# A gate group's copy moved ahead of its multiplication, top-k steps re-paced, and norm sums paired by column half, in a two-layer decoder on one core

## The chip, the cores and the metric

The kernel runs on one core of a Trainium2 chip. The metric is the device time of one execution in microseconds (us). The kernel before takes 2584.49 us, the median of 3 runs (2582.99 to 2586.38).

## The reference, cut to what matters

Two layers work on 256 tokens of 1024 features, all in float32. Each layer has a mixer (attention, a gated recurrence and retention, merged by gates and one output projection) and then PEER, a retrieval over 128 x 128 single-neuron experts. Each ends in a norm: `x = layer_norm(alpha * x + f(x))`, with mean and variance over the 1024 features of a token.

PEER computes `q = x @ wq`, scores it against two sets of 128 keys, takes the top 16 of each and the top 16 of the 256 sums, and weighs them by softmax. That gives, for each token and each of 8 heads, 16 expert numbers e and gates g. The output is `y = sum over (head, k) of gelu(U[e] . x) * g * V[e]`.

The kernel does not gather. It computes `gelu(U x)` for all 16384 experts, multiplies by a dense gate matrix G (expert by token, mostly zero), and multiplies by V.

## The kernel before, in words

**Jobs and splits.** The weights are cut into 408 jobs a layer, 128 x 1024 numbers (512 KB) each. `run` (line 498) goes through them in order. For a job it first prepares the weight of two jobs later (`ensure_split(i + LA)`, LA = 2): SyncE loads it to `raw` (4 buffers), ScalarE casts the high part `wh` (line 250), VectorE subtracts for the low part `wl` (line 259; for some mixer jobs partly GpSimd). `wh` and `wl` have 3 buffers each. Then it issues the job's matmuls (`mm_t`, lines 301 to 308: 16 with `wh`, then 8 with `wl`), then side work (`pump`), then what `post` returns (for a U pair the gelu, line 1163). Every engine has its own queue, worked off in the order in which the program issued the instructions.

**Side work and its pacing.** Side work is written as generators. At each `yield c` a step ends that is charged c credits. `pump(b)` (line 283) adds the budget b to the class's credit (at most b + 2) and takes steps as long as the credit is above zero. `drain` issues all that is left at once. Which step falls under which job thus follows from charges and budgets alone.

**The stages of a PEER sublayer.** 16 Q jobs give the queries, 128 U jobs (U0 to U127) the activations, 128 V jobs (V0 to V127) the output. Under Q and U0 to U61 runs the class topk: `head` (line 975) and `finish` (line 991), whose last part transposes the chosen numbers on TensorE (lines 1034 to 1041), behind a last reduction (line 1028). After U61 stands `drain("topk")`, after U63 the memory of this work is released. Under U64 to U127 runs the class g: `gbuild` (line 1077) makes G, 8 tokens at a time, in 32 steps b. VectorE writes one-hot matrices (`onehots`, lines 1088 to 1092; two buffers of each). TensorE multiplies them into a PSUM pair of two banks (`accpair`, two pairs in all; lines 1114 and 1115, 16 matmuls, called a group here). `use` reads the pair twice: VectorE multiplies the first half of the experts into the ring of activations (line 1099), ScalarE copies the other half to `ge` (line 1101) and sends it to DRAM (line 1102) for `gback` to fetch in the V stage. `act_prep` (line 1143) splits two activations for the V jobs; the first one needs all 32 multiplications.

In each step b the order is

```
one-hots of b+1; group b; use(b-1): line 1099, line 1101, line 1102
```

**Sums and norm.** `body_o` (line 913) and `vjob`/`vmm` (lines 1179 to 1194) collect the result in four banks, [token half t][column half n]. `ln_flow` (line 351) issues the last products of a quarter, then `ln_part` (line 346): VectorE adds the quarter to the residual (line 348) and takes its statistics (line 349). Dependencies are tracked by tile, so the two halves of a pair count as one: a matmul into one half waits until a read of the other half, issued earlier, is over.

Of the kernel before, what the change touches and what calls it, by code (L numbers as in the profile page):

```python
# [169 lines left out]
def build(ctx: ExitStack, tc: tile.TileContext, I, out, layers=LAYERS, dbg=None):  # L170
# [18 lines left out]
    def nm(s):  # L189
        uid[0] += 1  # L190
        return f"{s}_{uid[0]}"

    def mmps():
        return ps.tile([P, 512], F32, tag="mm", name=nm("mm"), bufs=2)
# [4 lines left out]
    def accpair():  # L199

        return ps.tile([P, 1024], F32, tag="acc", name=nm("acc"), bufs=2)

    def accps2():
        a = accpair()
        return [a[:, 0:512], a[:, 512:1024]]
# [292 lines left out]
    def run(jobs, body, budget, late=None):  # L498

        for job in jobs:
            i = J["i"]
            assert allj[i][1] == job, (allj[i], job)
            if job != late:
                ensure_split(i + LA)
            h, lo = parts.pop(i)
            post = body(job, h, lo)
            if job == late:
                ensure_split(i + LA)  # L510
            pump(budget)
            if post is not None:
                post()
            J["i"] += 1


    def mixer(l, mp, xdram, xnext):
# [395 lines left out]
        def body_o(job, h, lo):  # L913
            n, k2 = job[1], job[2]
            if k2 == 0:
                for t, o in enumerate(accps2()):
                    V["o"][t][n] = o
            accs = [V["o"][0][n], V["o"][1][n]]
            if (n, k2) == (1, 3):
                ln_flow(lambda t, n: mm_n(accs, h, lo, V["mh"], V["ml"], k2, True, (t,)), [1], V["o"],  # L920
                        2.0 * ALPHA, X, sts, 4.0 * EPS, l, 0, gb, L8(), mp, xnext)
                return None
            mm_n(accs, h, lo, V["mh"], V["ml"], k2, k2 == 3)

            def post():
                for t in range(2):
                    ln_part(t, n, V["o"][t][n], 2.0 * ALPHA, X, sts)
            return post if k2 == 3 else None
# [6 lines left out]
    def peer(l, jobs, pp, ra, xdram, xnext):  # L935
        pos = [0]

        def take(n):
            r = jobs[pos[0]:pos[0] + n]
            pos[0] += n  # L940
            return r
# [49 lines left out]
        def finish():  # L991

            e = tp.tile([P, 2, 8, 16], F32, tag="e", name=nm("e"))
            sm = tp.tile([P, 2, 8], F32, tag="esum", name=nm("esum"))
            nc.vector.tensor_tensor(e, cv, cv[:, :, :, 0:1].to_broadcast([P, 2, 8, 16]), op=ALU.subtract)
            a = tp.tile([P, 2, 2, 128], U32, tag="ab", name=nm("ab"))
            cf = ci.rearrange("p t h k -> p t (h k)")
            nc.vector.tensor_scalar(a[:, :, 0, :], cf, 4, None, op0=ALU.logical_shift_right)
            nc.vector.tensor_scalar(a[:, :, 1, :], cf, 15, None, op0=ALU.bitwise_and)
            af = tp.tile([P, 2, 2, 8, 16], F16, tag="af", name=nm("af"))  # L1000
            nc.vector.tensor_copy(af, a.rearrange("p t f (h k) -> p t f h k", h=8))
            xf = tp.tile([P, 2, 2, 8, 16], F16, tag="xf", name=nm("xf"))
            nc.vector.tensor_copy(xf, i12)
            yield 1.9
            nc.scalar.activation(e, e, AF.Exp)
            yield 2.0
            nc.vector.tensor_reduce(sm, e, axis=AX.X, op=ALU.add)
            nc.vector.reciprocal(sm, sm)
            nc.vector.tensor_scalar(sm, sm, GSCALE, None, op0=ALU.mult)
            nc.vector.tensor_tensor(e, e, sm[:, :, :, None].to_broadcast([P, 2, 8, 16]), op=ALU.mult)  # L1010
            yield 1.3
            sel = tp.tile([P, 2, 2, 128], F32, tag="sel", name=nm("sel"))
            prev = None
            for t in range(2):
                for hf in range(2):
                    eq = tp.tile([P, 8, 16, 16], F16, tag="q8", name=nm("eq"), bufs=2)
                    sh = [P, 8, 16, 16]
                    nc.vector.tensor_tensor(eq, af[:, t, hf, :, :, None].to_broadcast(sh),
                                            iota[:, None, None, 0:16].to_broadcast(sh), op=ALU.is_equal)
                    yield 2.3  # L1020
                    xb = xf[:, t, hf, :, None, :].to_broadcast(sh)
                    nc.vector.tensor_tensor(eq, eq, xb, op=ALU.mult)
                    yield 1.2
                    if prev is not None:
                        nc.vector.tensor_reduce(prev[0], prev[1], axis=AX.X, op=ALU.add)
                        yield 2.3
                    prev = (sel[:, t, hf, :], eq.rearrange("p h k j -> p (h k) j"))
            nc.vector.tensor_reduce(prev[0], prev[1], axis=AX.X, op=ALU.add)
            dump(f"cv{l}", cv)
            dump(f"sel{l}", sel)  # L1030
            dump(f"e{l}", e)
            yield 2.3
            yield 1.0
            pt = sideps()
            for t in range(2):
                for hf in range(2):
                    nc.tensor.transpose(pt[:, (2 * hf + t) * P:(2 * hf + t + 1) * P], sel[:, t, hf, :], ident)
            nc.scalar.copy(idxT[:, 0:2, :], pt.rearrange("p (f t) -> p f t", f=2))
            pg = sideps()
            for t in range(2):  # L1040
                nc.tensor.transpose(pg[:, t * P:(t + 1) * P], e[:, t].rearrange("p h k -> p (h k)"), ident)
            nc.scalar.copy(idxT[:, 2, :], pg[:, :S])
            nc.vector.tensor_tensor(idxT[:, 3, :], pg[:, :S], idxT[:, 2, :], op=ALU.subtract)
            yield 0.4
# [23 lines left out]
                add_side("topk", head(ct // 2))  # L1068
            return post if q else None
        V["q"] = set()  # L1070
        run(take(16), body_q, 1.4, ("Q", 1))
        add_side("topk", finish())

        def gbuild():
            def onehots(c):

                B = pp.tile([P, 4, P, 2], F16, tag="ohB", name=nm("ohB"), bufs=2)  # L1080
                A = pp.tile([P, 2, 4, P, 2], F16, tag="act", name=nm("ohA"), bufs=2)
                sh = [P, 4, P, 2]

                def of(q):
                    return idxT[:, q, 8 * c:8 * c + 8].rearrange("p (a k) -> p a k", k=2)[:, :, None, :].to_broadcast(sh)

                io = iota2[:, None, :, :].to_broadcast(sh)
                nc.vector.tensor_tensor(B, io, of(1), op=ALU.is_equal)  # L1088
                nc.vector.tensor_tensor(A[:, 1], io, of(0), op=ALU.is_equal)
                yield 1.4  # L1090
                nc.vector.tensor_tensor(A[:, 0], A[:, 1], of(2), op=ALU.mult)  # L1091
                nc.vector.tensor_tensor(A[:, 1], A[:, 1], of(3), op=ALU.mult)
                yield 1.4
                return A, B

            def use(b, pg):
                pv = pg.rearrange("p (k i) -> p i k", k=8)
                r = RA[:, :, 8 * b:8 * b + 8]
                nc.vector.scalar_tensor_tensor(r, pv[:, 0:64, :], 1.0 / GSCALE, r, op0=ALU.mult, op1=ALU.mult)  # L1099
                ge = pp.tile([P, 64, 8], F32, tag="ge", name=nm("ge"), bufs=2)  # L1100
                nc.scalar.activation(ge, pv[:, 64:128, :], AF.Copy, scale=1.0 / GSCALE)  # L1101
                nc.scalar.dma_start(gd[l, b], ge.rearrange("p i k -> p (i k)"))  # L1102

            cur = yield from onehots(0)
            prev = None
            for b in range(S // 8):
                A, B = cur
                if b + 1 < S // 8:
                    cur = yield from onehots(b + 1)
                pg = accpair()  # L1110
                for k in range(8):
                    o = pg[:, P * k:P * k + P]
                    w = B[:, k // 2, :, k % 2]
                    mm(o, lhsT=w, rhs=A[:, 0, k // 2, :, k % 2], start=True, stop=False)  # L1114
                    mm(o, lhsT=w, rhs=A[:, 1, k // 2, :, k % 2], start=False, stop=True)
                if prev is not None:
                    use(b - 1, prev)
                prev = pg
                yield 0.7
            yield 0.5  # L1120
            use(b, prev)
            yield 0.7
            act_prep(0)

        def gback(s):
# [37 lines left out]
                nc.scalar.activation(ring[s][:, i - 1:i + 1, :], pt.rearrange("p (a t) -> p a t", a=2), AF.Gelu)  # L1163
            return post if q else None

        run(take(62), body_u, 1.6)
        drain("topk")
        run(take(2), body_u, 1.6)
        tp.release()
        V["rb"] = tc.alloc_tile_pool(name=nm("rb"), bufs=4, reuse_waits="tile")  # L1170
        credit["g"] = 0.0
        add_side("g", gbuild())
        run(take(64), body_u, 1.9)
        drain("g")
        act_prep(0)

        V["y"] = [accps2(), accps2()]

        def vmm(j, t, n, h, lo):
            a = acts[j // 2]  # L1180
# [103 lines left out]
```

## Time and profile before

| | us |
|---|---|
| median of 3 runs | 2584.49 |
| profiled execution, its own time | 2581.74 |
| span of the profile, first to last instruction | 2580.0 |
| TensorE busy, share of the span | 2499.6, 97% |
| VectorE busy | 1834.0, 71% |
| ScalarE busy | 1174.8, 46% |
| mean granted clock of TensorE | 0.993 |

A busy share says which engine sets the pace on the whole. Where an engine waits, the idle time before an instruction is put down to the instruction that released it. The timeline gives start and duration of each instruction; a matmul's duration overlaps the next one's, so the pace of matmuls is read from their starts.

### The profile page before, as it was taken

How to read it: one execution, taken by the hardware profiler on the slowest of the kernel's cores; microseconds unless marked ns; L12 is line 12 of the kernel's file. 1: busy time of each engine (PE TensorE's matmuls, PEld its weight loads, DVE VectorE, ACT ScalarE, POOL GpSimd, SP SyncE). 2: the span in 40 equal slices, each digit the busy share in tenths (PEclk: the TensorE clock that was granted, in tenths of full speed). 3: DMA queues.
4: the chain of work that ended last, by engine and by line, in shares of the span. 5: the costliest groups of instructions: out<-in, count | busy, mean ns of one | idle time of the engine just before them, and what ended most of it. 6: DMA issues, size and time to landing. Idle time of an engine off the chain costs nothing.

```text
span 2580.0 us, 43337 instructions
## 1 busy us (share of the span) xinstructions
PE 2499.6 (97%) x17428; PEld 2310.0 (90%) x17428; DVE 1834.0 (71%) x2736; ACT 1174.8 (46%) x1480; POOL 282.8 (11%) x263
## 2 busy tenths in 40 slices
PE   8999999999999999999999999999999999999998
PEld 7989998999999888888789999989999998888886
DVE  7886656888877756665588756568888777567655
ACT  5444444444444344444454444444444444444443
POOL 0822110200000000000028220111000000000000
PEclk9999999999999999999999999999999999999999
DMA  6445565555545458666554455655555555586663
GB/s 232 156 149 168 168 214 178 191 177 176 170 169 187 167 197 256 226 227 226 166 205 148 156 167 173 213 171 188 173 181 174 175 178 174 190 260 228 223 226 131
DMA packets 165913, 485.96 MB, mean 188 GB/s; under 512 B 15056, under 2 KB 47952, under 8 KB 165072
## 3 DMA queue, kind: packets, MB, share of 16 engines
q1 hardware_dynamic: 119952, 434.43, 50.5%
q10 hardware_dynamic: 44800, 45.62, 5.5%
q8 instruction: 137, 2.24, 0.4%
q0 software_dynamic: 960, 3.15, 0.3%
q14 instruction: 64, 0.52, 0.1%
HBM read 462.16 MB, written 20.97 MB: 187 GB/s over the span
## 4 chain that ended last, share of the span: by engine, by line
PE 80%; DVE 11%; ACT 4%; issue 3%; POOL 1%; ACTq 1%; DVEq 0%; POOLq 0%
PE acc L1193 27%; PE mm L304 14%; PE mm L305 14%; PE mm L307 14%; DVE wl L259 5%; PE acc L334 3%; PE acc L335 2%; PE acc L338 2%; ACT wh L250 2%; ACT ge L1101 1%; DVE ring L1099 1%; DVE ohA L1091 1%; PE side L660 1%; ACTq L1102 1%; DVE ohB L1088 1%
## 5 line engine op out<-in xcount | busy, mean ns | idle before, releaser
L259 DVE TENSOR_TENSOR wl<-raw,wh 128x1024 fp32r<-128x1024 f32 (+3 forms) x817 | 1003.2, 1233 | 543.4 <-ACT wh L250 537.9
L250 ACT CAST wh<-raw 128x1024 fp32r<-128x1024 f32 (+1 forms) x817 | 850.5, 1048 | 563.1 <-PE acc L1193 349.3
L304 PE MATMUL mm<-xh,wh 128*128 128x256 f32 x3536 | 882.4, 287 | 11.7 <-ACT wh L250 11.7
L305 PE MATMUL mm<-xl,wh 128*128 128x256 f32 x3536 | 869.4, 283 | 0.0
L304 PEld LDWEIGHTS mm<-xh,wh 128*128 128x128 f32 x3536 | 679.9, 192 | 18.7 <-ACT wh L250 15.1
L305 PEld LDWEIGHTS mm<-xl,wh 128*128 128x128 f32 x3536 | 680.7, 193 | 0.5
L1193 PE MATMUL acc<-wh,act 128*128 128x512 f32 x2016 | 539.3, 389 | 0.0
L307 PE MATMUL mm<-xh,wl 128*128 128x256 f32 x3536 | 499.5, 284 | 5.4 <-DVE wl L259 3.2
L307 PEld LDWEIGHTS mm<-xh,wl 128*128 128x128 f32 x3536 | 456.9, 192 | 9.1 <-DVE wl L259 6.1
L1193 PEld LDWEIGHTS acc<-wh,act 128*128 128x128 f32 x2016 | 378.3, 188 | 78.4
L1193 PE MATMUL acc<-wl,act 128*128 128x512 f32 x1008 | 310.5, 389 | 0.0
L1193 PEld LDWEIGHTS acc<-wl,act 128*128 128x128 f32 x1008 | 189.2, 188 | 39.4
L1163 ACT ACTIVATE ring<-mm 128x512 f32<-128x512 f32 x128 | 76.3, 596 | 185.6 <-PE mm L307 178.2
L259 POOL TENSOR_TENSOR wl<-raw,wh 128x640 fp32r<-128x640 f32 (+2 forms) x50 | 68.7, 1385 | 740.8 <-ACT wh L250 696.6
L1101 ACT ACTIVATE ge<-acc 128x512 f32<-128x512 f32 x64 | 38.3, 598 | 222.6 <-DVE ring L1099 208.6
L376 POOL TENSOR_TENSOR lnv<-lnv,mhalf 128x1 f32<-128x1 f32 x8 | 5.6, 698 | 791.8 <-DVE lnv L378 783.0
L334 PE MATMUL acc<-wh,xh 128*128 128x512 f32 x224 | 91.5, 408 | 0.0
L343 DVE TENSOR_TENSOR act<-ring,act 128x512 fp32r<-128x512 f32 x128 | 87.7, 685 | 3.4 <-ACT act L342 3.4
L335 PE MATMUL acc<-wh,xl 128*128 128x512 f32 x224 | 87.6, 391 | 0.0
L1114 PE MATMUL acc<-ohA,ohB 128*128 128x128 f16 x512 | 67.4, 222 | 18.9 <-ACT ge L1101 18.7
L342 ACT CAST act<-ring 128x512 fp32r<-128x512 f32 x128 | 78.7, 615 | 1.7 <-issue 0.9
L643 POOL TENSOR_TENSOR qk<-w,w 128x256 f32<-128x256 f32 x40 | 51.4, 1285 | 182.4 <-DVE w L642 149.9
(246 smaller groups left out, 2342.4 us busy)
## 6 DMA issues: line engine op xcount, KB each, us to landing
raw<-in_ws SPq DMA_DIRECT2D x815, 512.0 KB, 3.3
gd<-ge ACTq DMA_DIRECT2D x64, 256.0 KB, 2.8
ring<-gd ACTq DMA_DIRECT2D x8, 2048.0 KB, 15.5
wg<-in_wgate SPq DMA_DIRECT2D x2, 1024.0 KB, 5.9
kk<-in_keys ACTq DMA_DIRECT2D x2, 1024.0 KB, 5.1
xd<-L POOLq DMA_DIRECT2D x8, 256.0 KB, 2.7
X<-xd ACTq DMA_DIRECT2D x2, 1024.0 KB, 5.7
dec<-in_dec ACTq DMA_DIRECT2D x2, 768.0 KB, 4.4
```

Source lines behind the costliest of these rows:

```text
L250: nc.scalar.copy(h[:, c], raw[:, c])
L259: eng.tensor_tensor(lo[:, c], raw[:, c], h[:, c].bitcast(F32), op=ALU.subtract)
L304: mm(o, lhsT=w, rhs=mh[:, koff + k, :], start=(k == 0), stop=False)
L305: mm(o, lhsT=w, rhs=ml[:, koff + k, :], start=False, stop=False)
L307: mm(o, lhsT=lo[:, base + k * P:base + (k + 1) * P], rhs=mh[:, koff + k, :], start=False, stop=(k == n - 1))
L334: mm(acc[t], lhsT=sh[:, k, ts], rhs=h[:, q * 512:(q + 1) * 512], start=first, stop=False)
L335: mm(acc[t], lhsT=sl[:, k, ts], rhs=h[:, q * 512:(q + 1) * 512], start=False, stop=False)
L342: nc.scalar.copy(h, src)
L343: nc.vector.tensor_tensor(lo, src, h.bitcast(F32), op=ALU.subtract)
L1114: mm(o, lhsT=w, rhs=A[:, 0, k // 2, :, k % 2], start=True, stop=False)
L1163: nc.scalar.activation(ring[s][:, i - 1:i + 1, :], pt.rearrange("p (a t) -> p a t", a=2), AF.Gelu)
L1193: mm(V["y"][t][n], lhsT=a[:, part, q, ts], rhs=w[:, n * 512:(n + 1) * 512], start=(j == 0 and x == 0), stop=False)
```

## The change

Four places are edited.

1. `gbuild`: `use` is split. `send` (ScalarE's copy and its DMA) is issued right behind the matmuls of its own group; `use` (VectorE's multiplication) comes in the next step, after the one-hots of the step behind it and ahead of the next group. The order becomes

```
one-hots of b+1; use(b-1): line 1099; group b; send(b): copy and DMA
```

2. End of the top-k work: the charge ahead of the transposes is 2.0 for 1.0, and the budgets are 1.5 for 1.4 (Q jobs) and 1.7 for 1.6 (U0 to U61), 1.85 for 1.9 under U64 to U127.
3. `body_o`: the sums of column half n = 1 go to two single-bank tiles (`mmps`) instead of a pair.
4. V stage: a pair holds the two token halves of one column half, where it held the two column halves of one token half.

```diff
-                for t, o in enumerate(accps2()):
+                for t, o in enumerate([mmps(), mmps()] if n else accps2()):
                     V["o"][t][n] = o
...
             yield 2.3
-            yield 1.0
+            yield 2.0
             pt = sideps()
...
-        run(take(16), body_q, 1.4, ("Q", 1))
+        run(take(16), body_q, 1.5, ("Q", 1))
...
+            def send(b, pg):
+                ge = pp.tile([P, 64, 8], F32, tag="ge", name=nm("ge"), bufs=2)
+                nc.scalar.activation(ge, pg.rearrange("p (k i) -> p i k", k=8)[:, 64:128, :], AF.Copy,
+                                     scale=1.0 / GSCALE)
+                nc.scalar.dma_start(gd[l, b], ge.rearrange("p i k -> p (i k)"))
+
             def use(b, pg):
-                pv = pg.rearrange("p (k i) -> p i k", k=8)
                 r = RA[:, :, 8 * b:8 * b + 8]
-                nc.vector.scalar_tensor_tensor(r, pv[:, 0:64, :], 1.0 / GSCALE, r, op0=ALU.mult, op1=ALU.mult)
-                ge = pp.tile([P, 64, 8], F32, tag="ge", name=nm("ge"), bufs=2)
-                nc.scalar.activation(ge, pv[:, 64:128, :], AF.Copy, scale=1.0 / GSCALE)
-                nc.scalar.dma_start(gd[l, b], ge.rearrange("p i k -> p (i k)"))
+                nc.vector.scalar_tensor_tensor(r, pg.rearrange("p (k i) -> p i k", k=8)[:, 0:64, :], 1.0 / GSCALE, r,
+                                               op0=ALU.mult, op1=ALU.mult)
...
-            for b in range(S // 8):
+            n = S // 8
+            for b in range(n + 1):
+                if b + 1 < n:
+                    nxt = yield from onehots(b + 1)
+                else:
+                    yield 2.8
+                if prev is not None:
+                    use(b - 1, prev)
+                    yield 0.7
+                if b == n:
+                    break
                 A, B = cur
-                if b + 1 < S // 8:
-                    cur = yield from onehots(b + 1)
-                pg = accpair()
+                cur = nxt
+                prev = accpair()
                 for k in range(8):
-                    o = pg[:, P * k:P * k + P]
+                    o = prev[:, P * k:P * k + P]
...
-                if prev is not None:
-                    use(b - 1, prev)
-                prev = pg
-                yield 0.7
-            yield 0.5
-            use(b, prev)
-            yield 0.7
+                send(b, prev)
             act_prep(0)
...
-        run(take(62), body_u, 1.6)
+        run(take(62), body_u, 1.7)
         drain("topk")
         run(take(2), body_u, 1.6)
...
-        run(take(64), body_u, 1.9)
+        run(take(64), body_u, 1.85)
         drain("g")
         act_prep(0)
-        V["y"] = [accps2(), accps2()]
+        yn = [accps2(), accps2()]
+        V["y"] = [[yn[n][t] for n in range(2)] for t in range(2)]
```

## Rows read from the trace of the kernel before

**Rows 1.** The page, part 1: busy time of each engine over the whole span, its share, and the number of instructions.

```profile
PE 2499.6 (97%) x17428; PEld 2310.0 (90%) x17428; DVE 1834.0 (71%) x2736; ACT 1174.8 (46%) x1480; POOL 282.8 (11%) x263
```

**Rows 2.** What TensorE (PE) waited for over the whole span: the waiting instruction, whom it waited for, us in total, times, longest.

```profile
PE acc L1114 <- ACT ge L1101: 18.7, 8, 4.5
PE mm L304 <- ACT wh L250: 11.7, 19, 0.9
PE acc L1184 <- DVE X L348: 4.3, 4, 1.2
```

**Rows 3.** The copy of line 1101 alone: what its engine, ScalarE, sat idle for before it (us, times).

```profile
  DVE ring L1099: 208.6, 58
```

**Rows 4.** TensorE in order of time (start us, duration us): the first matmul of some gate groups, layer 0 and, in the last row, layer 1.

```profile
703.12 0.23 PE L1114 MATMUL acc<-ohA,ohB 128*128 128x128 f16 x1
...
709.85 0.23 PE L1114 MATMUL acc<-ohA,ohB 128*128 128x128 f16 x1
...
736.79 0.23 PE L1114 MATMUL acc<-ohA,ohB 128*128 128x128 f16 x1
...
740.64 0.23 PE L1114 MATMUL acc<-ohA,ohB 128*128 128x128 f16 x1
...
852.73 0.22 PE L1114 MATMUL acc<-ohA,ohB 128*128 128x128 f16 x1
...
860.52 0.23 PE L1114 MATMUL acc<-ohA,ohB 128*128 128x128 f16 x1
...
1988.66 0.23 PE L1114 MATMUL acc<-ohA,ohB 128*128 128x128 f16 x1
```

**Rows 5.** The products of the V jobs (line 1193), one row for the start of the V stage in layer 0, one for layer 1: operation, count, duration ns, first and last start us within the stretch asked for.

```profile
L1193 PEld LDWEIGHTS acc<-wh,act x201: 187/188/192, 932.0 to 1000.0; 128*128 128x128 f32 x101
...
L1193 PEld LDWEIGHTS acc<-wh,act x242: 187/188/193, 2218.1 to 2299.9; 128*128 128x128 f32 x121
```

**Rows 6.** ScalarE (ACT) in order of time, in layer 0's stage with gate groups (start us, duration us, in brackets the idle time before and what ended it).

```profile
886.21 0.60 ACT L1101 ACTIVATE ge<-acc 128x512 f32<-128x512 f32 x1 [4.13 <-DVE ring L1099]
886.84 0.33 ACTq L1102 DMA_DIRECT2D gd<-ge  x1
887.26 1.05 ACT L250 CAST wh<-raw 128x1024 fp32r<-128x1024 f32 x1 [0.45 <-PE mm L307]
888.21 0.59 ACT L1163 ACTIVATE ring<-mm 128x512 f32<-128x512 f32 x1
...
920.66 0.62 ACT L342 CAST act<-ring 128x512 fp32r<-128x512 f32 x1 [0.40 <-ACT ge L1101]
```

**Rows 7.** VectorE (DVE) in the same stretch, same columns.

```profile
881.82 0.68 DVE L1088 TENSOR_TENSOR ohB<-iota,idxT 128x1024 f16<-128x1024 f16 x1
...
885.49 0.68 DVE L1099 SCALAR_TENSOR_TENSOR ring<-acc,ring 128x512 f32<-128x512 f32 x1
888.34 1.23 DVE L259 TENSOR_TENSOR wl<-raw,wh 128x1024 fp32r<-128x1024 f32 x1 [2.16 <-ACT wh L250]
```

**Rows 8.** Stretches of layer 0 around the last wait of that stage: us, busy time of each engine (instructions), granted TensorE clock, DMA share, GB/s.

```profile
911.00:915.00 4.00, 0.00 (x0) 0.00 (x0) 3.96 (x6) 1.07 (x2) 0.00 (x0) 1.00 0.38 140
915.00:918.00 3.00, 2.67 (x21) 2.67 (x21) 0.44 (x2) 1.92 (x3) 0.00 (x0) 0.53 0.93 325
```

**Rows 9.** TensorE in order of time at the end of the top-k work, layer 0 (first two rows) and layer 1.

```profile
683.15 0.38 PE L1037 MATMUL side<-ident,sel 128*128 128x128 f32 x2
...
690.64 1.12 PE L307 MATMUL mm<-xh,wl 128*128 128x256 f32 x8
...
1973.87 0.33 PE L1037 MATMUL side<-ident,sel 128*128 128x128 f32 x1 [2.32 <-DVE sel L1028]
...
1974.18 0.37 PE L304 MATMUL mm<-xh,wh 128*128 128x256 f32 x1
...
1976.18 1.12 PE L307 MATMUL mm<-xh,wl 128*128 128x256 f32 x8
```

**Rows 10.** What VectorE waited for in a stretch of top-k work under U jobs (560 to 640 us).

```profile
DVE wl L259 <- ACT wh L250: 7.8, 10, 1.7
```

**Rows 11.** The same stretch as a whole, columns as in group 8.

```profile
560.00:640.00 80.00, 80.00 (x671) 80.00 (x670) 69.95 (x203) 36.88 (x45) 4.34 (x7) 1.00 0.54 178
```

**Rows 12.** VectorE's sums of the norm behind the V stage, layer 0 (first two rows) and layer 1.

```profile
1279.24 0.69 DVE L348 SCALAR_TENSOR_TENSOR X<-X,acc 128x512 f32<-128x512 f32 x1 [1.02 <-PE acc L1184]
...
1283.50 0.69 DVE L348 SCALAR_TENSOR_TENSOR X<-X,acc 128x512 f32<-128x512 f32 x1 [1.03 <-PE acc L1184]
...
2564.97 0.69 DVE L348 SCALAR_TENSOR_TENSOR X<-X,acc 128x512 f32<-128x512 f32 x1 [1.02 <-PE acc L1184]
...
2569.23 0.69 DVE L348 SCALAR_TENSOR_TENSOR X<-X,acc 128x512 f32<-128x512 f32 x1 [1.03 <-PE acc L1184]
```

**Rows 13.** TensorE's last products of the V stage in layer 0.

```profile
1277.54 0.50 PE L1184 MATMUL acc<-wh,act 128*128 128x512 f32 x1 [1.11 <-DVE X L348]
...
1281.80 0.50 PE L1184 MATMUL acc<-wh,act 128*128 128x512 f32 x1 [1.22 <-DVE X L348]
```

**Rows 14.** The norm behind the mixer, layer 0: VectorE's sum of the last quarter, and TensorE's first product of that quarter.

```profile
443.77 0.69 DVE L348 SCALAR_TENSOR_TENSOR L<-L,acc 128x512 f32<-128x512 f32 x1 [0.53 <-PE acc L338]
...
442.07 0.50 PE L334 MATMUL acc<-wh,L 128*128 128x512 f32 x1 [1.19 <-DVE L L348]
```

**Rows 15.** TensorE early in the Q jobs of layer 1.

```profile
1755.03 2.08 PE L307 MATMUL mm<-xh,wl 128*128 128x256 f32 x8 [2.64 <-DVE wl L259]
```

## The prediction

> **What bounds the kernel now.** I read the busy line first: TensorE works 97% of the span, so what can be won are its gaps, some 80 us, and stretches in which it runs slowly [rows 1]. The waits of TensorE then say where the gaps are: ahead of gate groups, behind ScalarE's copy of an earlier group (18.7 us), ahead of U products, behind ScalarE's casts, and ahead of the last V products, behind VectorE's sums [rows 2]. Asking for the copy itself shows why it is late: ScalarE sat idle 208.6 us in front of it, 58 times, until VectorE's multiplication of the same pair was done [rows 3]. Each reads other elements, and yet they run one after the other.
>
> That wait closes a loop. The multiplication ends at 886.17, the copy starts at 886.21; the cast behind it comes at 887.26, and VectorE sits 2.16 us until it can subtract for that weight [rows 6, 7]. VectorE's side steps then delay the next multiplication, which delays the next copy and cast. While TensorE is not held, one group and two U jobs take 6.73 us and one group and one job 3.85 us, so a job is 2.88 us and a group 0.97 us; in the loop the same two jobs and group take 7.79 us [rows 4]. The worst wait, near the stage's end, leaves TensorE without work from 911 to 915 us, and it then runs at a granted clock of 0.53, near the lower of its levels (1.2 of 2.4 GHz), until about 918 [rows 8].
>
> **Part 1, copy ahead of multiplication.** From the first group to the first V product lie 61 U jobs and 32 groups: the first steps are charged 1.4 each at 1.9 a job, which puts group 0 behind U66. Unheld that is 61 x 2.88 + 32 x 0.97 = 206.7 us. It took 932.0 - 703.12 = 228.9 us in layer 0 and 2218.1 - 1988.66 = 229.4 us in layer 1 [rows 4, 5]. So 22.2 + 22.7 = **44.9 us** lie in waits and slow matmuls. How much is left?
>
> I walk one step. Let T be the end of group b, behind U job i. On ScalarE the copy runs at once; with its DMA issue it holds the queue 1.05 us (886.21 to 887.26), a gelu 0.5 us more, then the cast for job i+3 runs 1.05 us: done at T + 2.6 [rows 6]. TensorE has two jobs to do first and wants it at T + 5.76: 3.1 us to spare. On VectorE the one-hots of b+2 reuse the buffer that group b read, and so also wait until T (new: nothing was issued between); two of them take 1.3 us, then it waits for the cast, subtracts until T + 3.8; the `wl` products want that at T + 7.7. Its work per two jobs and a group is four one-hots (2.7 us), a multiplication (0.6) and two subtractions (2.3): 5.6 of 6.73 us [rows 7]. Group b+1 wants one-hots issued a whole step earlier, and the pair of group b-1, whose copy and multiplication were both issued before group b. So neither wait has a successor in the steady state. SyncE's loads wait for subtractions of four jobs back, which come no later than in the loop of today; the copy's DMA moves with it and is fetched a stage later; GpSimd does nothing here [rows 8]. By charges (2.8 + 31 x 2.8 + 2 x 2.8 + 32 x 0.7 = 117.6 against 64 x 1.85 = 118.4) the last multiplication falls under U127, where it fell under U123. Now it stands right ahead of the V stage: multiplication 0.68, cast of the first activations 0.62 and a like subtraction. Hidden wholly it costs 0, bare 2.0 us a layer [rows 6, 7]. The multiplication can run while TensorE is still in U127, so I take 0.5: 1.0 in all. Part 1: **-43.9 us**, at least -30 if only whole waits go.
>
> The Trainium skill, "PSUM — Partial Sum Buffer", section "PSUM bank collisions raise a hardware error", says that ScalarE and VectorE may not access one bank at the same time, reads included, and must be kept apart by semaphores. The 208.6 us agree. By that rule the wait is only turned round, VectorE now waiting for the copy; if that cost as much as today half of the time, the sum would be rival (a)'s.
>
> **Part 2, top-k.** Before, the charges leave the last reduction for the drain or just ahead of it, and the transposes stand right behind. Layer 0: from the first transpose to the `wl` products of U62 go 7.49 us; three transposes and the 16 `wh` products run 2.31 us in layer 1, so six and 16 need 2.62: 4.87 us lost. Layer 1 waits 2.32 us [rows 9]. With the new charges I get the reduction under U57 or U58 and the transposes two jobs later, U59 or U60: the reduction (2.3 us) has 5.76 us, the drain finds nothing. ScalarE's copies behind the transposes now hold it until U59 or U60 is done, as a gelu does behind every second job. **-7.2 us.** The price is 0.1 credit more per job on VectorE, about 0.1 us; it was idle 10 of 80 us there, 0.36 a job [rows 11], 7.8 of it waiting for casts, that is, ahead of TensorE [rows 10]. I cost it at 0, at most 62 x 0.1 = 6 us a layer if that lead is not there. In layer 1 the saved-up credit reaches 3.5 and now lets a third top-k step in under Q1, ahead of a subtraction; TensorE waits 2.64 us there already [rows 15]. The wait moves one job forward with the same VectorE work before it: 0, between -1 and +2.
>
> **Parts 3 and 4, norms.** Behind V, TensorE holds the second quarter of each pair until the sum of the first is read [rows 13], and VectorE then waits 1.02 and 1.03 us for it, in both layers [rows 12]. With a pair per column half, neighbouring quarters lie in different pairs; six products take about 1.5 us, a sum and its statistics 1.45 us, so VectorE goes through: 4 x 1.02 = **-4.1 us**, all on the chain to the next layer or to the end. Behind the mixer TensorE's 1.19 us go, but VectorE waited 0.53 us only [rows 14]: **-1.1 us** for two layers.
>
> **Sum.** 43.9 + 7.2 + 4.1 + 1.1 = 56.3 us off the profiled execution's 2581.74 us: 2525.4. The median of the runs lies 2.75 us above that execution, so I predict **2528 us** (-2.2%). A difference of 0.2%, 5 us, is about the least that a measurement of this kernel can tell from none.
>
> **Rivals.** *(a) The loop turns round.* VectorE now waits for TensorE (one-hot buffers) and for ScalarE (the pair), and passes that on through the subtractions. For it: the 2.16 us behind a late cast [rows 7]. Against: the 3.1 and 3.9 us to spare. If half of the stage's loss came back, 22 us: 2550.
>
> *(b) Top-k at the faster pace holds the subtractions up,* or still ends in the drain. The first: 2 x 6 us, 2540; the second: 7 us, 2535. Against: 0.36 us idle per job [rows 11].
>
> *(c) Slower: the copy blocks ScalarE's queue.* It cannot start before TensorE has done group b, so every cast behind it loses its lead. It decides once the cast for job i+3 ends later than T + 5.76, and eats the whole gain at 56.3 / 64 = 0.88 us lost in each of 64 steps, that is at T + 6.6 where I walk to T + 2.6. At 1.2 us a step, 77 us: 2605. For it: in the loop of today a held copy did make casts late (11.7 us) [rows 2]. Against: 4 us are missing.
> The same page, section "Engine vs sequencer instructions", states that ScalarE's and VectorE's queues are strictly first in, first out, which speaks against putting a waiting copy ahead of casts; rows 6, where the cast follows the held copy, agree.
>
> *(d) No change:* a new wait eats all of it, 2584.
>
> **Chances.** Forecast 0.80, (a) 0.08, (b) 0.07, (c) 0.03, (d) 0.02. The first three are faster by over 0.2%: 0.95; same 0.02, slower 0.03. The forecast's own bounds: nothing left ahead of V, a shorter wait in Q and a fast median of the runs (-7 us) against 2.0 us a layer ahead of V, 2 us in Q and some waits of part 1 kept (+12): 2521 to 2540. To hold (b) and most of (a), 2548 above.
>
> **What would show it.** Right: the copy waits for TensorE (line 1114 or 1115), no longer for line 1099; line 1114 has no wait on line 1101, and group starts lie 6.73 or 3.85 us apart to the end; line 1037 no wait on 1025 or 1028; line 1184 none on 348; mean clock nearer 1. Wrong: group starts still 7 to 8 us apart, waits of line 304 on line 250 that stay near 11.7 us or grow, of line 307 on 259 that grow, or a wait of several us ahead of the first V product.

## The result, and the profile after

The changed kernel takes 2527.69 us (median of 4 runs, 2526.77 to 2528.43) against 2583.74 us (4 runs): ratio 0.978, interval 0.977 to 0.980. Predicted were 2528 us, in 2521 to 2548. Its profiled execution took 2526.77 us, with a span of 2524.9 us against 2580.0.

Lines of the changed kernel: the copy is line 1098, the multiplication 1104, the group's matmuls 1128 and 1129, the V products 1193 (last jobs) and 1202.

The page, part 1, as in [rows 1]:

```profile
PE 2481.4 (98%) x17428; PEld 2301.5 (91%) x17428; DVE 1834.6 (73%) x2736; ACT 1177.1 (47%) x1480; POOL 283.0 (11%) x263
```

TensorE's waits over the span, as in [rows 2] (line waited for, us in total, times, longest):

```profile
PE acc L411 <- ACT L L381: 5.2, 2, 2.6
PE mm L307 <- DVE wl L259: 4.0, 2, 3.5
...
PE acc L1202 <- ACT act L342: 0.9, 2, 0.5
...
PE mm L304 <- ACT wh L250: 0.7, 1, 0.7
```

The waits of the groups on the copy, of the last V products on VectorE's sums and of the top-k transposes on their reductions are not in the list any more; that on line 250 fell from 11.7 to 0.7 us. What is new or longer is small: 0.9 us ahead of the V stage, 5.2 us ahead of the transposes behind the mixer (before 2.3: TensorE gets there earlier and waits for the same ScalarE work), 4.0 us on subtractions (before 3.2). ScalarE's idle time ahead of the copy, as in [rows 3]:

```profile
  PE acc L1129: 164.1, 64
```

It still waits, 64 times, but for the matmuls of its own group, and TensorE doesn't wait for it. First matmuls of groups in layer 0, as in [rows 4]:

```profile
700.97 0.23 PE L1128 MATMUL acc<-ohA,ohB 128*128 128x128 f16 x1
...
820.26 0.23 PE L1128 MATMUL acc<-ohA,ohB 128*128 128x128 f16 x1
...
827.00 0.23 PE L1128 MATMUL acc<-ohA,ohB 128*128 128x128 f16 x1
...
898.18 0.23 PE L1128 MATMUL acc<-ohA,ohB 128*128 128x128 f16 x1
```

and the first V products, as in [rows 5]:

```profile
L1202 PEld LDWEIGHTS acc<-wh,act x161: 186/188/189, 905.5 to 959.9; 128*128 128x128 f32 x161
```

From 820.26 to 827.00 are 6.74 us, and so it goes on: from 700.97 to 898.18 there are 31 steps with 58 jobs between, 58 x 2.88 + 31 x 0.97 = 197.1 us; measured 197.2.

Where the 55.1 us of span went, by stages cut at the same instructions of both traces (first Q product, first U job with gate groups, first V product; that U job starts three jobs ahead of the first group before, four jobs after):

| stage | before, us | after, us | difference | forecast |
|---|---|---|---|---|
| start to Q, layer 0 | 448.5 | 448.4 | -0.1 | 0 |
| Q and U0 to U63, layer 0 | 246.0 | 241.0 | -5.0 | -4.9 |
| U64 to U127, layer 0 | 237.5 | 216.1 | -21.4 | -21.7 |
| V, norm, and mixer and norm of layer 1 | 800.9 | 798.3 | -2.6 | -2.6 |
| Q and U0 to U63, layer 1 | 247.1 | 245.4 | -1.7 | -2.3 |
| U64 to U127, layer 1 | 238.1 | 216.1 | -22.0 | -22.2 |
| V, norm, end | 361.9 | 359.6 | -2.3 | -2.0 |

(The forecast's 0.5 us for the norm behind the mixer of layer 0 belongs to the first row and does not show there: from the start of VectorE's last subtraction to that of its last sum went 3.58 us before and 2.96 after, but the mixer ahead of them ran 0.6 us later in this execution.)

### The profile page after: what moved, and what is told of

Read it like the earlier page. It is cut to its first block, busy times and chain, and to the rows that moved or that the text cites. A ratio compares the mean times of both kernels' runs of the same rounds, so it can differ in the third digit from the quotient of the medians.

```text
span 2524.9 us, 43400 instructions
## 1 busy us (share of the span) xinstructions
PE 2481.4 (98%) x17428; PEld 2301.5 (91%) x17428; DVE 1834.6 (73%) x2736; ACT 1177.1 (47%) x1480; POOL 283.0 (11%) x263
## 4 chain that ended last, share of the span: by engine, by line
PE 93%; DVE 4%; issue 1%; POOL 1%; ACT 1%; ACTq 0%; POOLq 0%; DVEq 0%
PE acc L1202 27%; PE mm L304 17%; PE mm L307 17%; PE mm L305 17%; PE acc L334 2%; PE acc L335 2%; PE acc L338 2%; PE acc L1128 1%; DVE wl L259 1%; PE acc L1129 1%; PE side L660 1%; PE side L970 0%; POOL wl L259 0%; PE side L716 0%; PE side L709 0%
## 5 line engine op out<-in xcount | busy, mean ns | idle before, releaser
L1098 ACT ACTIVATE ge<-acc 128x512 f32<-128x512 f32 x64 | 38.4, 600 | 164.1 <-PE acc L1129 164.1
L338 PE MATMUL acc<-wl,xh 128*128 128x512 f32 x224 | 69.1, 390 | 0.0
```

Source lines behind the costliest of these rows:

```text
L338: mm(acc[t], lhsT=sh[:, k, ts], rhs=lo[:, q * 512:(q + 1) * 512], start=False, stop=(last and q == 1))
```

## The experiments

Each is timed against the kernel before on the same chip (2583.98 to 2584.8 us in median).

**One part at a time.** Three kernels carry one part each on the kernel before.

Copy alone (edit 1, and the budget 1.85 of edit 2):

> Part 1 alone on the kernel before. Theory (the parts are independent): the stage with gate groups loses its 43.4 us and nothing else moves, about 2540 us, ratio 0.983. Rival (the parts help each other): clearly less than 43 us here, 2550 us or more.

Measured 2538.39 us, ratio 0.983 (0.981 to 0.984).

Norms alone (edits 3 and 4):

> The two edits of the norms' sums alone on the kernel before. Theory: 4 x 1.02 + 2 x 0.53 = 5.2 us less, about 2578.5 us, ratio 0.998. Rival: the products were not what the sums' chain waited for, no difference.

Measured 2578.08 us, ratio 0.997 (0.997 to 0.998).

Top-k alone (edit 2, with the budget under U64 to U127 left at 1.9):

> The top-k charges and budgets alone on the kernel before. Theory: 7.2 us less, less the wait of the Q jobs in layer 1 that grew by 0.9 us: about 2577.5 us, ratio 0.9975. Rival: VectorE at the faster pace holds subtractions up, no gain or 2584 us and more.

Measured 2576.25 us, ratio 0.997 (0.996 to 0.998). The three gains, 46, 6.5 and 8.3 us, add up to 61 us where all together give 56 to 57; with intervals of some 4, 2.5 and 3 us either way that is no sign of parts that help or hinder each other. The copy's part is four fifths of the whole.

**Is it the place of the copy, or its order against the multiplication?** The change alters both. The first kernel swaps the order and leaves the place:

```diff
-                nc.vector.scalar_tensor_tensor(r, pv[:, 0:64, :], 1.0 / GSCALE, r, op0=ALU.mult, op1=ALU.mult)
                 ge = pp.tile([P, 64, 8], F32, tag="ge", name=nm("ge"), bufs=2)
                 nc.scalar.activation(ge, pv[:, 64:128, :], AF.Copy, scale=1.0 / GSCALE)
                 nc.scalar.dma_start(gd[l, b], ge.rearrange("p i k -> p (i k)"))
+                nc.vector.scalar_tensor_tensor(r, pv[:, 0:64, :], 1.0 / GSCALE, r, op0=ALU.mult, op1=ALU.mult)
```

> The kernel before with one thing changed: inside use, ScalarE's copy and its DMA are issued ahead of VectorE's multiplication, both in the old place and with the old budgets. Theory (the loop is closed by the order of the two readers): the copy finds its group done a step ago and no longer waits for VectorE; all waits of the stage go, 44.9 us, about 2539 us. Rival (the place of the copy, right behind its own group, is what matters): the stage stays near 229 us and the time within 10 us of 2584.

Measured 2538.22 us, ratio 0.982 (0.981 to 0.984): the same as the copy's part alone (the medians lie 0.2 us apart, the runs of each kernel spread over some 5.5 us). ScalarE's idle time ahead of the copy (line 1100 there):

```profile
  PE acc L1115: 4.6, 6
```

208.6 us on VectorE have become 4.6 us on TensorE, and VectorE in its turn waits for the copy only twice, 2.1 us in all. The groups of layer 0, in one row (x count, duration ns, first and last start us), and the first V products of that kernel:

```profile
L1114 PE MATMUL acc<-ohA,ohB x256: 218/218/231, 705.1 to 897.3; 128*128 128x128 f16 x128
```

```profile
L1193 PEld LDWEIGHTS acc<-wh,act x142: 187/188/192, 911.8 to 959.5; 128*128 128x128 f32 x142
```

From 705.1 to 911.8 are 206.7 us, which is the prediction's figure for 61 jobs and 32 groups without any wait. So a swap of three statements takes the whole loop away, the wait ahead of V included, since the last multiplication still falls under U123.

The second kernel does the reverse: the new place for both, but VectorE first.

```diff
                 if prev is not None:
                     use(b - 1, prev)
+                    send(b - 1, prev)
                     yield 0.7
...
-                send(b, prev)
```

> The changed kernel with the copy moved back behind the multiplication of its pair, both in the new place (after the one-hots, ahead of the next group). Theory (order of the readers): the loop is closed again, the copy waits for VectorE once per step, and 10 to 22 us per layer come back: 2545 to 2570 us. Rival (the place is what matters, each pair being read before the next group is issued): within 5 us of 2528.

Measured 2567.39 us, ratio 0.993 (0.992 to 0.995): 40 us of the gain are gone. The copy waits for VectorE again (idle time ahead of line 1098; another 79.0 us, 17 times, the view puts down to no engine), and TensorE for casts and for the first activations of the V stage:

```profile
  DVE ring L1104: 125.0, 42
```

```profile
PE mm L304 <- ACT wh L250: 18.0, 20, 2.2
PE acc L1202 <- ACT act L342: 8.4, 2, 4.2
```

Order, not place, closes the loop.

**How much spare time have the casts behind the copy?** The slower rival, (c), holds that a copy that waits at the head of ScalarE's queue makes the casts late. Two kernels repeat the copy, five times and eight times, each writing the same values, so that ScalarE is held longer (shown for five):

```diff
-                nc.scalar.activation(ge, pg.rearrange("p (k i) -> p i k", k=8)[:, 64:128, :], AF.Copy,
-                                     scale=1.0 / GSCALE)
+                for _ in range(5):
+                    nc.scalar.activation(ge, pg.rearrange("p (k i) -> p i k", k=8)[:, 64:128, :], AF.Copy,
+                                         scale=1.0 / GSCALE)
```

> The changed kernel with the copy of each group done five times over (same result). A test of the spare time: ScalarE is held some 2.0 to 2.4 us longer per step, so that the cast for job i+3 ends at about T + 4.6 to T + 5.0, against T + 5.76 when TensorE wants it. Theory: no difference beyond 3 us, 2528 to 2531. Rival (the casts have no such spare time): each us held shows, 64 x 1 us or more, 2590 us.

Measured 2534.93 us, ratio 0.981 (0.979 to 0.982): 7 us more than the changed kernel, where 0 to 3 were expected. ScalarE in that kernel, one step of layer 0:

```profile
840.87 3.12 ACT L1099 ACTIVATE ge<-acc 128x512 f32<-128x512 f32 x5 [0.67 <-PE acc L1130]
844.02 0.33 ACTq L1101 DMA_DIRECT2D gd<-ge  x1
844.45 1.05 ACT L250 CAST wh<-raw 128x1024 fp32r<-128x1024 f32 x1 [0.45 <-DVE ohA L1089]
```

The group ends at about 840.85, the cast at 845.50, T + 4.65, as expected, and no product waits for it: line 250 is not among TensorE's waits under these jobs, and the groups start 6.73 or 3.85 us apart to the end. The 7 us lie elsewhere, at the end of the stage, where the last copies hold two casts, with them VectorE's subtractions and the last multiplication, and so the cast of the first activations (0.9 us in the changed kernel):

```profile
PE acc L1203 <- ACT act L342: 6.0, 2, 3.0
```

That is 5.1 us more, and slow matmuls behind it (granted clock 0.63 from 907 to 910 us, 1.00 in the changed kernel). So a step has at least 2.5 us to spare (T + 4.65 against T + 2.15 in the changed kernel, below); the expectation had left out the end of the stage.

> The same with the copy done eight times over. ScalarE then has about 4.0 to 4.8 us of copies, 0.4 of DMA issue, 0.5 of gelu and two casts of 1.05, 7.0 to 7.8 us for each step of 6.73, and the cast ends past T + 5.76. Theory: TensorE waits for casts in nearly every step, 0.3 to 1.1 us x 64: 2547 to 2598 us. Rival (the queue's order never reaches TensorE): 2528.

Measured 2621.66 us, ratio 1.015 (1.013 to 1.016): slower than the kernel before, and above the expected range. ScalarE in order of time:

```profile
846.49 5.01 ACT L1099 ACTIVATE ge<-acc 128x512 f32<-128x512 f32 x8
851.53 0.33 ACTq L1101 DMA_DIRECT2D gd<-ge  x1
852.23 1.04 ACT L250 CAST wh<-raw 128x1024 fp32r<-128x1024 f32 x1 [0.73 <-ACT ge L1099]
853.18 0.59 ACT L1172 ACTIVATE ring<-mm 128x512 f32<-128x512 f32 x1
853.67 1.04 ACT L250 CAST wh<-raw 128x1024 fp32r<-128x1024 f32 x1
854.61 5.01 ACT L1099 ACTIVATE ge<-acc 128x512 f32<-128x512 f32 x8
```

Eight copies take 5.0 us (0.63 each, where 0.5 to 0.6 were reckoned). With two casts, the gelu and the DMA issue they fill the 8.1 us from 846.49 to 854.61, more than the 6.73 us that TensorE needs for a step. The copy at 846.49 starts 3.6 us after its group has ended (842.9): ScalarE is behind with its work. The groups, and TensorE's waits:

```profile
L1129 PE MATMUL acc<-ohA,ohB x256: 218/218/231, 700.1 to 937.4; 128*128 128x128 f16 x128
```

```profile
PE mm L304 <- ACT wh L250: 62.8, 59, 2.8
PE acc L1203 <- ACT act L342: 10.9, 2, 5.4
```

The last start in the first row is that of the last group's last matmul of this line, 0.8 us into the group. So 31 steps take 236.4 us where the changed kernel needs 197.2: 1.3 us a step, 78 us for both layers, and 10 us more ahead of V; the expectation had 0.3 to 1.1 us a step and nothing ahead of V.

Casts that come late do hold TensorE, then. But this kernel does not show the rival's mechanism: the amount of ScalarE's work makes the casts late, not a copy that waits at the head of its queue, for in layer 0 only the first copy waits for TensorE. That such a wait costs nothing is what the kernel with five copies shows: its copies waited for TensorE 24 times in layer 0, 18.7 us in all, and no step grew. From which lateness on a waiting copy would cost time is not shown.

**What else waits.** Two places of the changed kernel have grown: the Q jobs of layer 1, where saved-up credit lets three top-k steps in under Q1 (the wait was 2.64 us [rows 15]), and the V stage's start. TensorE and three stretches around the first of them (busy time of PE, PEld, DVE, ACT and POOL, then as in [rows 8]):

```profile
1723.80 1.57 PE L307 MATMUL mm<-xh,wl 128*128 128x256 f32 x8 [3.47 <-DVE wl L259]
```

```profile
1721.00:1724.00 3.00, 0.20 (x1) 0.20 (x2) 2.96 (x5) 0.18 (x1) 2.90 (x3) 1.00 0.23 87
1724.00:1727.00 3.00, 3.00 (x17) 3.00 (x17) 3.00 (x2) 0.87 (x1) 1.47 (x2) 0.57 0.70 246
1727.00:1730.00 3.00, 3.00 (x24) 3.00 (x23) 2.90 (x11) 0.59 (x2) 0.00 (x0) 0.86 0.95 266
```

After the wait the granted clock is 0.57, near the lower of the two levels, then 0.86; the wait costs more than its 3.47 us. The first kernel resets the credit:

```diff
         V["q"] = set()
+        credit["topk"] = 0.0
...
-        run(take(64), body_u, 1.85)
+        run(take(64), body_u, 1.9)
```

> The changed kernel with the top-k credit set to zero ahead of the Q jobs (so that layer 1 starts as layer 0 does, with one step under Q1, not three) and budget 1.9 for 1.85 under U64 to U127. Theory: the wait of 3.5 us in layer 1's Q jobs shrinks to the 0.5 us of layer 0, and the two waits of 0.5 us ahead of the V stage go: 4 us less than the changed kernel, about 2524 us. Rival (the same VectorE work stands before those subtractions in any order): 2527 us.

Measured 2524.07 us (2523.54 to 2527.77), ratio 0.977 (0.976 to 0.979); the range reaches into that of the changed kernel, so the gain of 3.6 us is not clear of noise. The sum came out, the mechanism only in part: the wait ahead of V is gone, but of the two waits on subtractions the long one is 2.6 us still, as before the change. Behind it the granted clock stays at 1.00 (1724 to 1730 us), where it fell to 0.65 behind the wait of 2.64 us in the kernel before (1754 to 1757 us).

```profile
PE mm L307 <- DVE wl L259: 3.2, 2, 2.6
```

So the credit was not the whole reason. VectorE is late behind the norm by itself, and its subtractions are slow there. The same instruction in the changed kernel, early in these Q jobs and from 1727.2 us on:

```profile
L259 DVE TENSOR_TENSOR wl<-raw,wh x4: 1637/2218/2309, 1709.8 to 1723.7; 128x1024 fp32r<-128x1024 f32 x4
...
L259 DVE TENSOR_TENSOR wl<-raw,wh x11: 1204/1206/1227, 1728.6 to 1758.8; 128x1024 fp32r<-128x1024 f32 x11
```

Four of them take 1.6 to 2.3 us each, the later eleven 1.2 us. In the first stretch GpSimd is at work on the end of the norm (lines 440 and 441; 2.90 of 3 us in the stretch from 1721), in the second it does nothing. No run takes GpSimd's work away, so that it is the cause is not shown. What can be tried is whether TensorE pays for any top-k step that stands ahead of a subtraction there. The next kernel starts these steps later and makes up for it under the U jobs:

```diff
         V["q"] = set()
+        credit["topk"] = -6.0
...
-        run(take(62), body_u, 1.7)
+        run(take(62), body_u, 1.85)
...
-        run(take(64), body_u, 1.85)
+        run(take(64), body_u, 1.9)
```

> The changed kernel with the top-k credit set to -6 ahead of the Q jobs (first top-k step under Q4 or Q5 instead of Q1), budget 1.85 for 1.7 under U0 to U61 to make up for it, and 1.9 for 1.85 under U64 to U127. Theory (VectorE's backlog behind the norm, with top-k steps ahead of subtractions, is what TensorE waits for in layer 1's Q jobs): that wait, 2.6 us with the credit at zero, goes, and so does the 0.5 us of layer 0: 2520 us. Rival (VectorE is slow there by itself, or the faster pace holds subtractions up later): 2524 us or more.

Measured 2519.48 us (2518.19 to 2520.61), ratio 0.975 (0.974 to 0.976). It beats both kernels: the changed one, run beside it, came to 2527.29 us.

> The changed kernel once more, on the same chip as the other two, to compare with: 2527.7 us.

TensorE's waits from 1690 to 1800 us in the kernel with late top-k steps, and one stretch of its Q jobs:

```profile
PE acc L411 <- ACT L L381: 2.6, 1, 2.6
PE mm L326 <- DVE xl L437: 0.5, 1, 0.5
PE mm L304 <- ACT qT L1056: 0.3, 1, 0.3
PE acc L411 <- DVE L L384: 0.3, 1, 0.3
```

```profile
1719.00:1722.00 3.00, 3.00 (x28) 3.00 (x28) 2.02 (x9) 1.53 (x2) 2.68 (x3) 1.00 0.85 295
```

No wait on line 259 is left, and from 1712 us on TensorE is busy without a gap at full clock, though the subtractions are as slow as before. The first Q product to the last copy of Q results (line 1066) of layer 1 took 56.2 us in the changed kernel (1703.8 to 1760.0) and 50.1 here (1702.4 to 1752.5). Of these 6.1 us 0.9 are eight products of the scores (line 970) that now fall under U jobs, so the Q jobs gave back 5.2 of the 7.8 us.

Last, the swap in the old place with all the rest:

> The kernel before with the two readers swapped in the old place (old budget 1.9 there), the two norm edits, the top-k charges and budgets of the changed kernel, and the top-k credit set to zero ahead of the Q jobs. Theory (the place of the copy is worth nothing beyond the order): as fast as the changed kernel with the credit reset, 2524 us. Rival (the new place adds something that shows only without the other waits): 2528 us or more.

Measured 2525.2 us (2523.91 to 2527.28), ratio 0.977 (0.976 to 0.979), against 2524.07 and the same ratio in the new place, on another chip; the ranges overlap. The new place adds nothing that these runs can tell.

## Why the prediction was right

**The number.** That the median came within 0.3 us of 2528 is luck in part. The profiled execution became 55.0 us shorter, 1.3 less than the sum, and the median lies 0.9 us above it, where 2.75 us were added; the two misses cancel.

**The loop and its price.** Right. The working took the unheld pace from group starts of the kernel before and charged all that was over it to the loop: 44.9 us, less 1.0 ahead of V. The stage became 43.4 us shorter. What made it come out so well is that the price was not read from TensorE's listed waits (30 us of idle time) but from the pace, which also holds the slow matmuls behind a wait and the short gaps.

**The walk of one step.** Right, with more to spare. ScalarE and VectorE of the changed kernel, one step of layer 0 (group b ends at about 861.75):

```profile
861.79 0.60 ACT L1098 ACTIVATE ge<-acc 128x512 f32<-128x512 f32 x1 [2.28 <-PE acc L1129]
862.42 0.33 ACTq L1100 DMA_DIRECT2D gd<-ge  x1
862.85 1.05 ACT L250 CAST wh<-raw 128x1024 fp32r<-128x1024 f32 x1 [0.45 <-ACT ge L1098]
864.72 0.60 ACT L1171 ACTIVATE ring<-mm 128x512 f32<-128x512 f32 x1 [0.82 <-PE mm L307]
```

```profile
861.79 0.69 DVE L1088 TENSOR_TENSOR ohB<-iota,idxT 128x1024 f16<-128x1024 f16 x1 [0.31 <-PE acc L1129]
862.40 0.68 DVE L1089 TENSOR_TENSOR ohA<-iota,idxT 128x1024 f16<-128x1024 f16 x1
863.93 1.22 DVE L259 TENSOR_TENSOR wl<-raw,wh 128x1024 fp32r<-128x1024 f32 x1 [0.84 <-ACT wh L250]
865.07 0.68 DVE L1091 TENSOR_TENSOR ohA<-ohA,idxT 128x1024 f16<-128x1024 f16 x1
865.79 0.69 DVE L1092 TENSOR_TENSOR ohA<-ohA,idxT 128x1024 f16<-128x1024 f16 x1
866.40 0.68 DVE L1104 SCALAR_TENSOR_TENSOR ring<-acc,ring 128x512 f32<-128x512 f32 x1
```

The copy starts with the group's end, and the cast is done at 863.90, T + 2.15 (walked: T + 2.6, with a gelu between that here falls behind). The one-hots wait for the group, the subtraction ends at T + 3.4 (walked: 3.8). The multiplication at 866.40 waits for nobody, ScalarE least of all. The Trainium skill, page "PSUM — Partial Sum Buffer", section "PSUM bank collisions raise a hardware error", says that ScalarE and VectorE must not read one bank in the same partitions at the same time. The trace agrees in that the two readers stay ordered, as the 208.6 us before and the 125.0 us of the kernel with VectorE first bear out; no run here lets them read at once. With the copy first and a step between them the order costs no time.

**Ahead of V.** 0.5 us a layer taken, 0.45 measured (0.9 in all). The 0.5 was a choice between 0 and 2.0, not a walk to the end, so that it came so close is luck as well.

**Top-k.** Right in the main. The reduction starts at 674.43, the transposes behind it at 680.16, without a wait:

```profile
674.43 2.28 DVE L1028 TENSOR_REDUCE sel<-eq 128x128 f32<-128x2048 f16 x1
```

```profile
680.16 0.60 PE L1037 MATMUL side<-ident,sel 128*128 128x128 f32 x4
```

Layer 0 gained 5.0 us (4.9 forecast), layer 1 only 1.7 (2.3). The step that was off is the third top-k step under Q1: put at 0, between -1 and +2; the wait there grew from 2.64 to 3.47 us. With it one of the signs named for a wrong prediction, growing waits of line 307 on line 259, did appear (3.2 to 4.0 us in all), but in these Q jobs and not under U jobs. Nor did the working see that VectorE's subtractions take up to 2.3 us there.

**Norms.** VectorE goes through the sums without waiting (layer 0, behind V):

```profile
1250.31 0.68 DVE L348 SCALAR_TENSOR_TENSOR X<-X,acc 128x512 f32<-128x512 f32 x1
1251.03 0.69 DVE L349 BATCH_NORM_STATS2 lnst<-X 128x6 f32<-128x512 f32 x1
1251.64 0.67 DVE L348 SCALAR_TENSOR_TENSOR X<-X,acc 128x512 f32<-128x512 f32 x1
...
1253.45 0.68 DVE L348 SCALAR_TENSOR_TENSOR X<-X,acc 128x512 f32<-128x512 f32 x1
...
1254.77 0.67 DVE L348 SCALAR_TENSOR_TENSOR X<-X,acc 128x512 f32<-128x512 f32 x1
```

The second sum (line 348) follows the first by 1.33 us, with nothing between but the statistics, and from the second to the fourth are 3.13 us against 4.26 [rows 12]. Behind the mixer TensorE's gain went into a longer wait for ScalarE (5.2 for 2.3 us), as the working had it, which counted VectorE's 0.53 us only; measured are the 0.6 us a layer from the last subtraction to the last sum (3.58 to 2.96 us in layer 0, 3.57 to 2.95 in layer 1).

**The rivals.** (a) fell: no step paid. (b) fell: no new wait under U jobs. (c) fell: the copy does wait at the head of ScalarE's queue, 164.1 us in all, but the casts behind it are needed so much later that even 2.5 us more cost no step anything. Its loss of 1.2 us a step was an assumed size; that eight copies gave 1.3 is a matter of how many were chosen.

## What to carry to other kernels

When two engines read the same PSUM tile and are kept in order, issue first the reader whose queue feeds others, and last the reader that nobody waits for; here the swap alone is worth 1.8%. Price a stage with recurring waits from the unheld pace of its steps, not from listed waits. Where an engine comes late out of a serial stretch, such as a norm, hold side work back until its regular work has caught up (here 5.2 us of the Q jobs of layer 1).

## What the runs showed that was not expected

The Q jobs of layer 1 gave back 5.2 us once a wait of 3.47 us in them was gone; part of the rest is the granted clock of 0.57 in the 3 us behind it. The prediction had taken that wait as given. VectorE's subtraction of 128 x 1024 took up to 2.3 us in the changed kernel while GpSimd was busy, though not each time, and 1.2 us wherever GpSimd was idle. Eight copies of 128 x 512 in a row took 0.63 us each, no less than one by itself (0.60).
